# A two-layer hybrid mixer: decay rows through DRAM, and four pieces of work in another order

## The chip, the cores and the metric

The kernel runs on one core of one Trainium2 chip. The metric is device time in microseconds for one execution. The engines named below are PE (TensorE, matrix products), DVE (VectorE), ACT (ScalarE), POOL (GpSimd) and SP (SyncE, which here only issues DMAs).

## The reference

The input is one sequence of 512 tokens with 1024 features. Each of two layers has four attention-like branches of 256 features (FOX with a learned decay, DIL with dilated windows, RET a retention, MLA with low-rank queries and keys), a sigmoid gate of 1024 features for each, an output product, and a gated feed-forward block of 2816. Everything is float32.

```python
def hybrid_mixer(h, w_in, b_forget, ret_gn_gain, mla_q_norm, mla_kv_norm, w_uq, w_ukv, w_gate, w_branch, w_out):
    (fq, fk, fv, ff, dq, dk, dv, rq, rk, rv, rg, cq, ckv, kr) = jnp.split(h @ w_in, IN_OFFSETS, axis=-1)
    log_f = jax.nn.log_sigmoid((ff + b_forget).astype(jnp.float32))
    decay = jnp.cumsum(log_f, axis=1).transpose(0, 2, 1)
    o_a = causal_block_attention(heads(fq, FOX_HEADS), heads(fk, FOX_HEADS), heads(fv, FOX_HEADS),
                                 HEAD_DIM ** -0.5, decay)   # s + decay[query] - decay[key], causal softmax
    o_b = dilated_attention(heads(dq, DIL_HEADS), heads(dk, DIL_HEADS), heads(dv, DIL_HEADS))
    o_c = retention(...)                                     # then a norm over each head, gain, silu(rg)
    o_d = causal_block_attention(q_mla, k_mla, ...)          # q, k from rms_norm(cq) @ w_uq, rms_norm(ckv) @ w_ukv
    branches = jnp.stack([merge_heads(o_a), merge_heads(o_b), o_c, merge_heads(o_d)], axis=2)
    gates = jax.nn.sigmoid(h @ w_gate).reshape(B, S, N_BRANCH, D_MODEL)
    merged = jnp.sum(jnp.einsum('bsnw,nwd->bsnd', branches, w_branch) * gates, axis=2)
    return merged @ w_out

for l in range(2):                                           # reference()
    h = rms_norm(x, g_pre_mix[l])
    x = x + rms_norm(hybrid_mixer(h, ...), g_post_mix[l])
    h = rms_norm(x, g_pre_ffn[l])
    f = (jax.nn.silu(h @ w_ffn_gate[l]) * (h @ w_ffn_up[l])) @ w_ffn_down[l]
    x = x + rms_norm(f, g_post_ffn[l])
```

## The kernel before

All activations stay in SBUF; the weights are streamed from DRAM. A float32 product is made of three products of rounded parts (`mm3`, L527 to L531: high by high, high by low, low by high, 512 tokens wide). Each weight tile therefore goes through three steps: SP loads it into one of three `raw` buffers, ACT rounds it into `whi` (L289 for most of the layer, L404 for the feed-forward's wider tiles), and DVE subtracts to get `wlo` (L290, L405). The conversion runs two units ahead of the products.

The main stream is PE's list of weight products: `latents`, the projections, the gates, the output block, the feed-forward. The branches run beside it as generators: after each 6.5 main products, one step of the branch in progress is taken (a step ends at a `yield`). So a further `yield` in a branch puts 6 to 7 more main products between two of its steps. Inside regions marked as ordered the written order holds; elsewhere a scheduler orders each engine's instructions by the dependencies. PE, DVE, ACT, POOL and SP each run their own list strictly in order: an instruction that waits holds up what is behind it. PSUM has two pools of four banks each, `acc` for the main stream and `b` for the branches and other short work.

The places that the change touches:

- `running_sum` (L982) makes FOX's running sums of the log decay, `cum`, one column for each of four token blocks and four heads, by two fp32 matmuls (L989, L990). `attention` needs each head's sums also as a row along the free axis, the same in all 128 partitions: `spread(h)` makes them with four fp32 matmuls against the identity (L648) into a `b` bank, and ACT copies them to `dk[h]` (L651). `make_bias` (L660, DVE) turns `dk[h]` and `cum` into the bias of one block of scores. Behind it follow L681 (minimum and bias, DVE), L683 (exponential, ACT), L690 and L691 (reciprocal on DVE, product on POOL), and the transposes L698 on PE.
- `group_norm` (L826) is retention's norm over heads: sums by PE (L840), an inverse root in some 13 small DVE steps (`factor`, L538 to L546, L846, L848), five yields, and then transposes of the factors (L858) on PE.
- `latents` (L1180) ends the low-rank product. After the last `ps_d` product (`mm3` into a `b` bank) DVE makes the factors of two small norms from the squares that ACT summed (the norm chain, L1205 to L1212, with one root on ACT, L552), and L1215 to L1219 read the four `acc` banks of the latents token block by token block, scaled by them. The transposes of MLA's preparation (L891, L897) need the result. `next_spread` (ACT's copy L1078) and the conversion of the next two weight tiles (`w_conv`: L289, L290) stand inside the `ps_d` loop.
- `quarter_products` (L488) runs the feed-forward's products as seven groups over quarter blocks, with four banks from one pool: `b` for even, `acc` for odd column groups g. In layer two, `to_tokens` (L1723) turns the residual with transposes into `b` banks (L1729), which ACT copies out (L1732).
- `finish` (L1736) is the down product of layer two and what follows: the last of its seven products (n = 6) runs over 11 tiles of k (steps of two), the first eight for both token halves, the others for one half after the other. Each half then goes through a square sum on ACT (L1817), L1819, a root, and L1830 on DVE, and to DRAM.

## Time and profile before

| | us |
|---|---|
| median of 3 runs | 1676.44 (1675.61 to 1676.55) |
| the profiled execution | 1679.01 |
| its span | 1677.2 |
| PE busy in it | 1649.3 |
| DVE, ACT, POOL busy | 1130.8, 851.0, 358.7 |
| mean granted clock of TensorE | 0.997 |

The profile shows one execution. A timeline row gives the start of a group of like instructions, its duration, engine, line and operation, and in brackets how long the engine had been idle before it and what released it. Products on PE overlap, so the time that one takes from the queue is the distance between two starts and not its printed duration.

### The profile page before, as it was taken

The page shows a single profiled execution, that of the slowest core. Times are in us where ns is not written, and L with a number is a line of the kernel's source. Part 1 is how long each engine was busy: PE and PEld are TensorE (multiplying, and loading weights), DVE is VectorE, ACT ScalarE, POOL GpSimd, SP SyncE. Part 2 cuts the span into 40 slices and gives each one's busy share as a digit, 9 for nine tenths or more (in the row PEclk, how much of TensorE's full clock was granted, in tenths as well). Part 3 has the DMA queues.
Part 4 walks back from the last instruction along what each step waited for, and adds up shares of the span by engine and source line. Part 5 has one row for each costly group of instructions (what it writes and reads, how often), then busy time and mean ns, then how long its engine had stood idle before and what let it go on. Part 6 is the DMA issues. An engine that isn't in the chain of part 4 may idle for free.

```text
span 1677.2 us, 26506 instructions
## 1 busy us (share of the span) xinstructions
PE 1649.3 (98%) x9746; PEld 1463.0 (87%) x9746; DVE 1130.8 (67%) x2165; ACT 851.0 (51%) x1682; POOL 358.7 (21%) x400
## 2 busy tenths in 40 slices
PE   8999999999999999999989999999999999999997
PEld 7898888788899999988878988888888989999876
DVE  6657676556469777762286576766565687777897
ACT  6666554323456555553265665533234565555665
POOL 0244333432130000000122343333321300000000
PEclk9999999999999999999999999999999999999999
DMA  5644225667735777443245452256665247775572
GB/s 205 173 107 139 82 82 175 170 169 182 213 87 144 189 186 184 95 154 99 76 148 160 108 145 76 90 175 168 173 161 178 75 137 191 186 183 153 189 234 92
DMA packets 93698, 248.88 MB, mean 148 GB/s; under 512 B 11521, under 2 KB 23041, under 8 KB 93569
## 3 DMA queue, kind: packets, MB, share of 16 engines
q1 hardware_dynamic: 72768, 205.24, 39.0%
q0 software_dynamic: 20800, 41.95, 13.6%
q8 instruction: 77, 1.26, 0.3%
q14 instruction: 53, 0.43, 0.1%
HBM read 220.93 MB, written 31.46 MB: 150 GB/s over the span
## 4 chain that ended last, share of the span: by engine, by line
PE 89%; DVE 6%; issue 2%; ACT 1%; DMA 1%; POOL 1%; DVEq 0%; SPq 0%; POOLq 0%
PE acc L529 15%; PE acc L530 15%; PE acc L531 15%; PE b L503 4%; PE b L505 4%; PE b L504 4%; PE acc L505 3%; PE acc L504 3%; PE acc L503 3%; PE b L752 2%; PE b L672 2%; PE b L698 1%; PE acc L1891 1%; PE acc L1893 1%; PE acc L1892 1%
## 5 line engine op out<-in xcount | busy, mean ns | idle before, releaser
L529 PE MATMUL acc<-a,whi 128*128 128x512 f32 (+1 forms) x1254 | 485.5, 387 | 0.0
L531 PE MATMUL acc<-a,wlo 128*128 128x512 f32 (+1 forms) x1254 | 475.2, 379 | 0.0
L530 PE MATMUL acc<-a,whi 128*128 128x512 f32 (+1 forms) x1227 | 465.3, 379 | 0.0
L289 ACT CAST whi<-raw 128x512 fp32r<-128x512 f32 (+3 forms) x398 | 214.0, 576 | 346.5 <-PE acc L530 174.7
L290 DVE TENSOR_TENSOR wlo<-raw,whi 128x512 fp32r<-128x512 f32 (+3 forms) x398 | 271.9, 713 | 133.4 <-ACT whi L289 132.7
L531 PEld LDWEIGHTS acc<-a,wlo 128*128 128x128 f32 x1254 | 236.3, 188 | 44.7
L529 PEld LDWEIGHTS acc<-a,whi 128*128 128x128 f32 x1254 | 237.1, 189 | 40.0 <-issue 1.0
L530 PEld LDWEIGHTS acc<-a,whi 128*128 128x128 f32 x1227 | 231.9, 189 | 38.9 <-issue 1.0
L405 DVE TENSOR_TENSOR wlo<-raw,whi 128x1024 fp32r<-128x1024 f32 x132 | 157.8, 1195 | 69.0 <-ACT whi L404 67.3
L404 ACT CAST whi<-raw 128x1024 fp32r<-128x1024 f32 x132 | 135.4, 1027 | 126.6 <-PE b L504 48.0
L503 PE MATMUL b<-a,whi 128*128 128x256 f32 x560 | 158.7, 283 | 0.0
L504 PE MATMUL b<-a,whi 128*128 128x256 f32 x560 | 158.5, 283 | 0.0
L505 PE MATMUL b<-a,wlo 128*128 128x256 f32 x560 | 158.5, 283 | 0.0
L1302 DVE TENSOR_TENSOR a<-acc,a 128x512 f32<-128x512 f32 x64 | 44.1, 689 | 140.0 <-PE acc L531 140.0
L503 PE MATMUL acc<-a,whi 128*128 128x256 f32 x448 | 126.8, 283 | 0.0
L504 PE MATMUL acc<-a,whi 128*128 128x256 f32 x448 | 126.8, 283 | 0.0
L505 PE MATMUL acc<-a,wlo 128*128 128x256 f32 x448 | 126.8, 283 | 0.0
L503 PEld LDWEIGHTS b<-a,whi 128*128 128x128 f32 x560 | 107.5, 192 | 0.2
L504 PEld LDWEIGHTS b<-a,whi 128*128 128x128 f32 x560 | 107.5, 192 | 0.0
L505 PEld LDWEIGHTS b<-a,wlo 128*128 128x128 f32 x560 | 107.5, 192 | 0.0
L333 POOL DMA_DIRECT2D raw<-wts x36 | 32.3, 896 | 345.8 <-DMA raw<-wts 140.6
L521 ACT CAST a<-a 128x512 fp32r<-128x512 f32 (+1 forms) x143 | 76.6, 567 | 51.8 <-DVE a L1094 10.7
(282 smaller groups left out, 3203.6 us busy)
## 6 DMA issues: line engine op xcount, KB each, us to landing
raw<-wts SPq DMA_DIRECT2D x257, 512.0 KB, 3.9
raw<-wts POOLq DMA_DIRECT2D x36, 512.0 KB, 6.9
a<-a SPq DMA_DIRECT2D x120, 128.0 KB, 2.3
sums<-wts POOLq DMA_DIRECT2D x30, 512.0 KB, 6.6
raw<-sums SPq DMA_DIRECT2D x20, 512.0 KB, 4.1
raw<-wts SPq DMA_DIRECT2D x35, 256.0 KB, 2.9
sums<-sums POOLq DMA_DIRECT2D x10, 512.0 KB, 3.7
a<-xT SPq DMA_DIRECT2D x16, 256.0 KB, 6.0
```

What stands on the lines that cost most here:

```text
L289: todo.append(lambda hi=hi, src=src, n=n: nc.scalar.copy(hi[:, :n], src))
L290: todo.append(lambda hi=hi, lo=lo, src=src, n=n: (lo_engine or nc.vector).tensor_sub(lo[:, :n], src, hi[:, :n].bitcast(F32)))
L404: self.nc.scalar.copy(hi, src)
L405: self.nc.vector.tensor_sub(lo, src, hi.bitcast(F32))
L503: mm(o, hi[:, c], x[k][0], start=first, stop=False, skip_group_check=i in (2, 3, 4, 6))
L504: mm(o, hi[:, c], x[k][1], start=False, stop=False, skip_group_check=i in (2, 3, 4, 6))
L505: mm(o, lo[:, c], x[k][0], start=False, stop=k == 3, skip_group_check=i in (2, 3, 4, 6))
L521: nc.scalar.copy(hi, src)
L529: mm(out, w[0], x[0], start=start, stop=False)
L530: mm(out, w[0], x[1], start=False, stop=False)
L531: mm(out, w[1], x[0], start=False, stop=stop)
L1302: nc.vector.tensor_mul(z, ps, self.rB)
```

## The change

`spread(h)` becomes one DMA. `running_sum` makes the sums a second time, as 16 rows of 128 tokens (two more fp32 matmuls, with their operands exchanged), ACT copies them from PSUM, SP writes them to a DRAM tile `cum_rows`, and each head reads its four rows back into all 128 partitions. `running_sum` and the start of FOX's attention get one more `yield` each. `group_norm` waits seven yields and not five. The norm chain of `latents` moves into the `ps_d` loop, ahead of `next_spread` and `w_conv`. In layer two the column groups of the feed-forward exchange `b` and `acc`, and so do the banks of `finish`. In the last product of `finish` the steps from k = 6 on, not from k = 8 on, are held back and run one token half after the other.

```diff
--- before.py
+++ after.py
@@ -52,6 +52,7 @@
 HQ = 3
 OPS = 3
 LATE = 8
+LAST = 6
 AHEAD = 2
 FH = FT // 2
 LAST_K = tuple((k, min(2, FH - k)) for k in range(0, FH, 2))
@@ -643,12 +644,9 @@
         cum = self.cum if kind == FOX else None
 
         def spread(h):
-            ps = self.ps("b")
-            for t in range(4):
-                nc.tensor.matmul(ps[:, 128 * t:128 * t + 128], cum[:, 4 * t + h:4 * t + h + 1].to_broadcast([128, 128]),
-                                 self.con("ident"), start=True, stop=True)
             dk[h] = self.a()
-            self.defer(lambda: nc.scalar.copy(dk[h], ps))
+            rows = self.cum_rows.rearrange("(t h) c -> h t c", h=4)[h:h + 1]
+            nc.sync.dma_start(dk[h].rearrange("p (t c) -> p t c", t=4), rows.to_broadcast([128, 4, 128]))
 
         n = len(items)
         biases = {}
@@ -719,6 +717,7 @@
 
         if kind == FOX:
             spread(0)
+            yield
             yield
             make_bias(0)
         for x in range(n + LG + 2):
@@ -847,11 +846,8 @@
             r = self.rsqrt(v, 8)
             nc.vector.tensor_copy(rw.rearrange("p (g c) -> p g c", c=64), r.unsqueeze(2).to_broadcast([128, 8, 64]))
         self.defer(factor)
-        yield
-        yield
-        yield
-        yield
-        yield
+        for _ in range(7):
+            yield
         rb = self.ps("b")
         for t in range(4):
             ts = slice(128 * t, 128 * t + 128)
@@ -989,7 +985,18 @@
         nc.tensor.matmul(ps[:, 0:16], self.con("tri"), nl, start=True, stop=False)
         nc.tensor.matmul(ps[:, 0:16], self.con("ones"), before, start=False, stop=True)
         self.cum = self.cp.tile([128, 16], F32, tag="cum", name="cum")
-        self.defer(lambda: nc.vector.tensor_copy(self.cum, ps[:, 0:16]))
+        rows = self.ps("b")
+        nc.tensor.matmul(rows[0:16, 0:128], nl, self.con("tri"), start=True, stop=False)
+        nc.tensor.matmul(rows[0:16, 0:128], before, self.con("ones"), start=False, stop=True)
+        self.cum_rows = self.dram.tile([16, 128], F32, tag="cum", name="cum")
+
+        def out():
+            nc.vector.tensor_copy(self.cum, ps[:, 0:16])
+            t = self.a()
+            nc.scalar.copy(t[0:16, 0:128], rows[0:16, 0:128])
+            nc.sync.dma_start(self.cum_rows, t[0:16, 0:128])
+        self.defer(out)
+        yield
         yield
         yield
 
@@ -1198,18 +1205,18 @@
                         nc.scalar.activation(junk[:, 0:n], self.ps_l[t][:, o:o + n], AF.Square,
                                              accum_out=ss[:, c:c + 1])
             if k == (QT1 if l else QT):
+
+                nc.vector.tensor_mul(t8[:, 0:4], self.rT, self.rT)
+                for i, n in ((0, 256), (4, 128)):
+                    nc.vector.scalar_tensor_tensor(v[:, i:i + 4], ss[:, i:i + 4], 1.0 / n, t8[:, 0:4], op0=ALU.mult, op1=ALU.mult)
+                nc.vector.tensor_scalar_add(v, v, RMS_EPS)
+                for _ in self.root(v, f, t8):
+                    pass
+                for i in (0, 4):
+                    nc.vector.tensor_mul(f[:, i:i + 4], f[:, i:i + 4], self.rT)
                 self.next_spread()
                 self.w_conv(self.wi)
             self.mm3(ps_d, (w[0][k], w[1][k]), u[k], k == 0, k == KT - 1)
-
-        nc.vector.tensor_mul(t8[:, 0:4], self.rT, self.rT)
-        for i, n in ((0, 256), (4, 128)):
-            nc.vector.scalar_tensor_tensor(v[:, i:i + 4], ss[:, i:i + 4], 1.0 / n, t8[:, 0:4], op0=ALU.mult, op1=ALU.mult)
-        nc.vector.tensor_scalar_add(v, v, RMS_EPS)
-        for _ in self.root(v, f, t8):
-            pass
-        for i in (0, 4):
-            nc.vector.tensor_mul(f[:, i:i + 4], f[:, i:i + 4], self.rT)
         for t in range(4):
             o, r = self.ps_l[t], self.rT[:, t:t + 1]
             nc.vector.tensor_scalar_mul(cq[t // 2][:, 256 * (t % 2):256 * (t % 2) + 256], o[:, 0:256], f[:, t:t + 1])
@@ -1695,7 +1702,7 @@
                     stt(z[1][:, h0], o, -1.0, z[1][:, h0], op0=ALU.mult, op1=ALU.mult)
                     keep(z[1])
 
-            yield from self.quarter_products(ops, ("b", "acc")[g % 2], {
+            yield from self.quarter_products(ops, ("b", "acc")[(g + (xt is not None)) % 2], {
                 0: copy(0), 1: copy(1), 2: copy(2), 3: after_v, 4: after_r, 5: after_a12, 6: after_a22})
         self.wi = self.q_end
         return hid
@@ -1804,7 +1811,7 @@
                 f, k, nk = todo.popleft()
                 ready.append(f(k, nk))
 
-        chain, other, late = ([self.ps(t), self.ps(t)] for t in ("acc", "acc", "b"))
+        chain, other, late = ([self.ps(t), self.ps(t)] for t in ("b", "b", "acc"))
         banks = (chain, other, late, late, chain, chain, chain)
         e = {}
         y, xt = {}, {}
@@ -1871,7 +1878,7 @@
                     for i in range(nk):
                         beside[n](k + i)
                 held.append((k, nk, ready.popleft(), w))
-                if k >= LATE:
+                if k >= (LATE if n < 6 else LAST):
                     continue
                 self.block(banks[n], held.pop(), (0, 1), first, grouped)
             for t in range(2):
```

The new kernel's line numbers differ by up to seven, and the orders below carry each kernel's own.

PE at the start of FOX in layer one, before (`cum` is the tile of sums, `acc` rows are the main stream):

```order
L530 MATMUL acc<-a,whi 128x512
L531 MATMUL acc<-a,wlo 128x512
L648 MATMUL b<-ct,cum 128x128 x4
L529 MATMUL acc<-a,whi 128x512
L530 MATMUL acc<-a,whi 128x512
L531 MATMUL acc<-a,wlo 128x512
```

and after, behind `running_sum`'s first two matmuls:

```order
L532 MATMUL acc<-a,wlo 128x512
L985 MATMUL b<-sm_1548,ct 128x16
L986 MATMUL b<-sm_2260,ct 128x16
L989 MATMUL b<-ct,sm_1548 16x128
L990 MATMUL b<-ct,sm_2260 16x128
L530 MATMUL acc<-a,whi 128x512
L531 MATMUL acc<-a,whi 128x512
```

The four matmuls of a spread are gone from between the main products, and two wide ones (16 rows by 128) stand behind the two that made `cum`; up to FOX's first scores (L672, now L670) there are 33 main products where there were 21, and up to the first L698 (now L696) 68 where there were 51.

SP at the same place, before:

```order
L1099 DMA a<-a 64x512 x6
L258 DMA raw<-wts 128x512
L258 DMA raw<-wts 128x1024 x2
L258 DMA raw<-wts 128x512
L258 DMA raw<-wts 128x1024 x2
```

and after (`cum<-a` is the write to DRAM, `a<-cum` the broadcast reads of the four heads):

```order
L1106 DMA a<-a 64x512 x5
L997 DMA cum<-a 16x128
L1106 DMA a<-a 64x512
L259 DMA raw<-wts 128x512
L649 DMA a<-cum 128x4x128 x2
L259 DMA raw<-wts 128x1024
L649 DMA a<-cum 128x4x128
L259 DMA raw<-wts 128x1024
L649 DMA a<-cum 128x4x128
```

The write waits for ACT's copy and the first two reads for the write; the reads of the third and fourth head stand behind loads of the main stream.

DVE at the end of `latents` in layer two, before (`sm` names are small tiles, L290 is the weights' subtraction, L1215 the first read of the latents' banks):

```order
L562 TENSOR_TENSOR sm_9098<-sm_9098,sm_9099 128x4
L290 TENSOR_TENSOR wlo<-raw,whi 128x512 x2
L1205 TENSOR_TENSOR sm_9075<-sm_9098 128x4
L1207 SCALAR_TENSOR_TENSOR sm_9073<-sm_9072,sm_9075 128x4 x2
L1208 TENSOR_SCALAR sm_9073<-sm_9073 128x8
L554 RECIPROCAL sm_9074<-sm_9075 128x8
L556 TENSOR_TENSOR sm_9075<-sm_9074 128x8
L558 TENSOR_TENSOR sm_9075<-sm_9075,sm_9073 128x8
L560 TENSOR_SCALAR sm_9075<-sm_9075 128x8
L562 TENSOR_TENSOR sm_9074<-sm_9074,sm_9075 128x8
L1212 TENSOR_TENSOR sm_9074<-sm_9074,sm_9098 128x4 x2
L1215 TENSOR_SCALAR a<-acc,sm_9074 128x256
```

and after:

```order
L1209 TENSOR_TENSOR sm_9062<-sm_9085 128x4
L1211 SCALAR_TENSOR_TENSOR sm_9060<-sm_9059,sm_9062 128x4 x2
L1212 TENSOR_SCALAR sm_9060<-sm_9060 128x8
L555 RECIPROCAL sm_9061<-sm_9062 128x8
L557 TENSOR_TENSOR sm_9062<-sm_9061 128x8
L559 TENSOR_TENSOR sm_9062<-sm_9062,sm_9060 128x8
L561 TENSOR_SCALAR sm_9062<-sm_9062 128x8
L563 TENSOR_TENSOR sm_9061<-sm_9061,sm_9062 128x8
L1216 TENSOR_TENSOR sm_9061<-sm_9061,sm_9085 128x4 x2
L291 TENSOR_TENSOR wlo<-raw,whi 128x512 x2
L1222 TENSOR_SCALAR a<-acc,sm_9061 128x256
```

The chain now stands ahead of the two subtractions (L291 there) and no longer between them and the reads of the banks (L1222 there). In layer one it is the same, and there PE's first `acc` products stand ahead of the transposes L891 (now L887): 18 of them, where there were none.

PE at the first column group of layer two's feed-forward, before:

```order
L530 MATMUL acc<-a,whi 128x512
L531 MATMUL acc<-a,wlo 128x512
L1729 MATMUL b<-ct,a 128x128 x16
L503 MATMUL b<-a,whi 128x256
L504 MATMUL b<-a,whi 128x256
L505 MATMUL b<-a,wlo 128x256
```

and after:

```order
L504 MATMUL acc<-a,whi 128x256
L505 MATMUL acc<-a,whi 128x256
L506 MATMUL acc<-a,wlo 128x256
L1736 MATMUL b<-ct,a 128x128 x16
L504 MATMUL acc<-a,whi 128x256
L505 MATMUL acc<-a,whi 128x256
```

The group's products now write `acc`, and 15 of them stand ahead of the transposes L1729 (now L1736).

## Rows read from the trace of the kernel before

**Rows 1.** The page, part 1: busy us, share of the span, instructions.
```profile
PE 1649.3 (98%) x9746; PEld 1463.0 (87%) x9746; DVE 1130.8 (67%) x2165; ACT 851.0 (51%) x1682; POOL 358.7 (21%) x400
```

**Rows 2.** Waits of PE: us in total, times, longest us.
```profile
PE b L891 <- DVE a L1215: 4.1, 2, 3.1
...
PE b L858 <- DVE a L848: 2.1, 2, 1.5
...
PE b L1729 <- ACT a L1732: 1.4, 1, 1.4
```

**Rows 3.** Timeline, FOX first spread: start us, us, engine, line, operation, count.
```profile
180.91 1.05 PE L648 MATMUL b<-ct,cum 128*128 128x128 f32 x8
...
181.72 0.48 PE L529 MATMUL acc<-a,whi 128*128 128x512 f32 x1
...
182.04 0.39 PE L530 MATMUL acc<-a,whi 128*128 128x512 f32 x1
...
182.27 0.39 PE L531 MATMUL acc<-a,wlo 128*128 128x512 f32 x1
```

**Rows 4.** DMA issues: operation, count, KB each, median us to landing.
```profile
raw<-wts SPq DMA_DIRECT2D x35, 256.0 KB, 2.9
...
a<-tab SPq DMA_DIRECT2D x12, 256.0 KB, 3.9
...
a<-a SPq DMA_DIRECT2D x32, 64.0 KB, 2.0
...
a<-uq SPq DMA_DIRECT2D x4, 256.0 KB, 5.9
...
sums<-a POOLq DMA_DIRECT2D x24, 0.0 KB, 3.6
```

**Rows 5.** Timeline, all engines, FOX's start in layer one.
```profile
183.17 0.71 ACT L289 CAST whi<-raw 128x256 fp32r<-128x256 f32 x2
...
185.83 0.73 DVE L660 SCALAR_TENSOR_TENSOR a<-a,cum,ct 128x128 f32<-128x128 f32 x2
...
191.41 0.38 POOL L691 TENSOR_SCALAR a<-a,sm 128x128 f32<-128x128 f32 x1 [6.73 <-DVE sm L690]
...
193.06 0.30 PE L698 MATMUL b<-ct,a 128*128 128x128 f32 x1
```

**Rows 6.** Timeline, PE and DVE, end of latents in layer one.
```profile
32.99 0.15 DVE L1205 TENSOR_TENSOR sm<-sm 128x4 f32<-128x4 f32 x1
...
34.33 0.39 PE L531 MATMUL b<-a,wlo 128*128 128x512 f32 x1
...
36.02 0.21 DVE L1219 SCALAR_TENSOR_TENSOR sm<-acc,sm,vt 128x4 f32<-128x4 f32 x1
...
36.38 0.47 PE L529 MATMUL acc<-a,whi 128*128 128x512 f32 x1
```

**Rows 7.** Timeline, ACT, DVE and PE, end of latents in layer two.
```profile
867.07 0.58 ACT L1078 COPY a<-b 128x512 f32<-128x512 f32 x1
...
871.55 0.48 DVE L1215 TENSOR_SCALAR a<-acc,sm 128x256 f32<-128x256 f32 x1
...
872.19 0.52 PE L891 MATMUL b<-ct,a 128*128 128x128 f32 x2 [3.09 <-DVE a L1215]
```

**Rows 8.** Windows: stretch, us, PE (x), PEld, DVE, ACT, POOL, PEclk, DMA, GB/s.
```profile
872.70:875.80 3.10, 3.10 (x9) 2.48 (x8) 3.10 (x13) 2.18 (x4) 0.00 (x0) 0.51 0.00 0
...
1374.00:1378.00 4.00, 2.56 (x20) 1.89 (x18) 3.31 (x5) 3.44 (x7) 0.86 (x1) 1.00 0.76 165
```

**Rows 9.** Timeline, DVE, retention's norm steps in layer one.
```profile
294.70 3.43 DVE L542 TENSOR_TENSOR sm<-sm 128x8 f32<-128x8 f32 x1
```

**Rows 10.** Timeline, PE and DVE, first quarter group of layer two.
```profile
1376.14 2.12 PE L1729 MATMUL b<-ct,a 128*128 128x128 f32 x16 [1.44 <-ACT a L1732]
...
1381.01 0.69 DVE L1650 TENSOR_TENSOR a<-a,acc 128x512 f32<-128x512 f32 x1 [3.55 <-ACT a L1642]
```

**Rows 11.** Timeline, DVE, the last steps, after the last matmul.
```profile
1670.66 0.68 DVE L1819 SCALAR_TENSOR_TENSOR a<-acc,a 128x512 f32<-128x512 f32 x1
```

## The prediction

> **What bounds the kernel now.** I read the page's busy times first. PE is busy 1649.3 us of a span of 1677.2 [rows 1], so about 28 us are idle, and a change can only pay by taking work from PE's queue, by closing one of its few waits, or by raising its clock. Then I read PE's waits. The reader is to see that the list is short: the three waits that this change touches are 4.1, 2.1 and 1.4 us [rows 2], 7.6 us in all. What lies on DVE, ACT, POOL or SP costs nothing until PE comes to it, so each part below is priced by the moment at which PE arrives against the moment at which the operand is there. One fp32r product of 512 columns takes PE 0.23 us from start to start (182.04 to 182.27 [rows 3]).
>
> **FOX's running sums: the matmuls that go.** One spread is four fp32 matmuls. It holds PE from 180.91 to 181.72, 0.81 us, and the first product behind it takes 0.32 instead of 0.23 [rows 3]: 0.90 us a spread. There are eight (four heads, two layers): −7.2. The new running_sum adds two fp32 matmuls over 128 columns in each layer. A spread's four are of the same width, so two cost half of 0.81, 0.41 us; they stand right behind two fp32 matmuls that are there already, so no further change of format is paid. Two layers: +0.8. Together **−6.4**. The ACT copies of the spreads go too, but no PE wait hangs on them.
>
> **FOX's running sums: the round trip that comes.** The trace of before has neither this small write nor a broadcast read, so I bound them. ACT's copy of the 16 rows stands right behind the second cast of L289, which ends near 183.9 [rows 5]; the write is issued near 184.1. The nearest row for it is the 64 KB move on the same queue, 2.0 us; the longest for something small is 3.6, on POOL's queue [rows 4]. I take 2.0: the rows are there near 186.1, and SP, which waited for that, issues the first two reads. A read is 256 KB in runs of 512 bytes, four for each partition. The nearest rows of that size are 2.9 for a weight load, 3.9 for a table, and at the far end 5.9 for uq [rows 4]. I take 3.5, between the first two, since the reads go out behind a weight load and in a pair: dk of the first head lands near 189.6. From the first bias (185.83) to the end of POOL's L691 (191.41 + 0.38) the kernel before needs 5.96 us [rows 5], so the first normalised block would be there near 195.6.
>
> When does PE ask for it? Before, the first L698 comes at 193.06 [rows 5] with 51 products between L990 and itself; the order of after has 68. The 17 more are 3.9 us (17 by 0.23); two spreads less are −1.8 and the new pair is +0.4: 195.6. So the two extra yields buy almost exactly what the round trip costs, and the slack is about nothing. Counted in the same way from the order, the second head has some 1.4 us to spare, the third some 0.2 (SP issues its read behind a 512 KB load that waits for a free buffer), and the fourth 2.5. While a bias waits for its dk, DVE's queue stands: behind L660 (658 now) are queued the wlo subtractions of the main stream's weights, two units ahead, and then the reciprocals that POOL needs, so a late read reaches PE at L698 first. I price it at 0.3 a layer, **+0.6**. The ends: at 2.9 us nothing; at 5.9, 2.4 us late on the first and the third head of both layers, +9.6 more. A write of 3.6 alone delays the first head, 1.6 us a layer, +3.2.
>
> A rule speaks to this. The Trainium skill, "DMA: Bandwidth & Descriptors", section "Anatomy of one DMA — SWDGE (gpsimd) path", gives a transfer a fixed part of about 2.0 us beside its bytes at 436 GB/s, which for 256 KB makes an estimate of 2.6 us; by it the term would be 0 and the sum −13.2. It is written for the gpsimd path, and the table loads of this trace take 3.9, so the rows decide here.
>
> **Latents, layer one.** PE ends the ps_d products with the one at 34.33, could go on at 34.56, and starts the first acc product at 36.38 [rows 6]: 1.82 us, with three transposes in it. The norm chain on DVE starts at 32.99, behind two subtractions of L290, and the first token block's last reader of its acc bank is L1219, which ends at 36.23 [rows 6]. The change puts the chain ahead of those subtractions, into time in which DVE waited for ACT; with its 2.2 us gone from behind them, L1219 ends near 34.0 to 34.4, before PE wants the bank. In the order of after PE goes straight from ps_d to acc products, and the transposes stand in fours behind 18 of them. They still cost three times 0.13 us (sixteen take 2.12 [rows 10]): 1.8 less 0.4, **−1.4**. Its ends: −1.8 and −0.6, if ACT's casts come late by the chain's square root.
>
> **Latents, layer two.** Here the transposes stay ahead of the acc products and PE waits 3.09 us until 872.19 [rows 7]. The chain leaves DVE's queue behind the subtractions, but its square root now stands on ACT ahead of the copy of L1078, which began at 867.07 [rows 7]. The chain can't start before the squares that ACT ends just there, and its first steps and the root take some 0.7, so that copy would begin near 867.8; the casts and the subtractions behind it come 0.75 later, so of the chain's 2.1 us about 1.2 are gained: L1215 near 870.4 instead of 871.55, L891 near 871.0. There is a second part. After the wait the granted clock is 0.51 for 3.1 us, that is the lower level, 1.2 GHz, with PE busy throughout [rows 8]: work of 1.6 us at full clock, 1.5 lost. Around the wait of 1.44 us at L1729 the granted clock stays 1.00 [rows 8]. The new wait is 1.8 to 1.9, nearer to that than to 3.09, so I take the clock as held: −1.2 −1.5 = **−2.7**; the other end −1.2.
>
> **Retention's norm steps.** L858 waits 1.5 and 0.6, 2.1 in all [rows 2], for the inverse root; one DVE step of it stretches to 3.43 us [rows 9]. Two more yields put 15 and 18 more products ahead of L858, at least 3.4 us, more than either wait: **−2.1**. The steps behind it come later by as much, and the gate groups that need them are more than a group away. Ends: −2.1 and −1.
>
> **Banks of layer two.** PE waits 1.44 at L1729 for ACT's copies, which free the b banks, and the first group's products, on b too, stand behind [rows 10]. On acc, 15 half-width products (half of 0.23 each, 1.8 us) go ahead of the transposes in the order of after and cover it. But the last of the four acc banks is freed by L1650, which DVE ends at 1381.70 [rows 10]; PE now comes to that bank after 36 half-width products and 16 transposes, 6.2 us after 1374.7, near 1380.9. So 0.8 of the 1.44 comes back: **−0.6**, ends −1.4 and +0.2.
>
> **The last steps.** With six instead of eight kept common, more of the last product is done for one token half first. In the order the first half's last matmul is nine from the end before and after, since it needs the last weights in both, and DVE's L1819 of the second half starts at 1670.66 behind the first half's work [rows 11]. **0**; if that work moved ahead of PE's end, up to −1.3, and if a bank were held, +0.3.
>
> **The sum.** −6.4 + 0.6 − 1.4 − 2.7 − 2.1 − 0.6 + 0 = −12.6. Against the profiled execution (1679.0 us, of which the span is 1677.2) this is 1666.4. That execution lies 2.6 above the median of 1676.4, so the predicted median is **1664 us** (1663.8). A measurement of this kernel can tell about 0.2%, 3.4 us, from no change.
>
> **The rivals.** (a) *The reads land late.* For it: 512-byte runs, a pair of reads at once beside a weight load, and rows up to 5.9 [rows 4]. Against it: the loads of that size from plain rows take 2.9. At 5 us each the first and the third head lose 1.5 in each layer, +6: 1670. (b) *Waits only move.* The latents' clock still falls (+1.5), L1650 gives back all of L1729's wait and more (+1), and latents of layer one keeps 0.9 of its wait behind the casts. For it: each freed PE comes earlier to DVE's subtractions, and DVE is 67% busy [rows 1]. That is +3.4: 1667. (c) *Slower than before.* The same mechanism as (a) alone, at L660: every microsecond of landing over 3.5 costs four, so the gain of 12.6 is gone at 3.5 + 12.6/4 = 6.6 us, and at 7.5 the kernel is 0.2% slower, 1680. For it speaks only that no broadcast read from DRAM is in the trace; against it that uq's 5.9 is as slow as a transfer of that size gets in the rows [rows 4]. The same section of the Trainium skill says that completion can be surprisingly long when a write goes to HBM, as the 16 rows do; by that the write, not the reads, would be late, and the first head alone would pay. No row here shows it. (d) *Part of the change does nothing.* The bank swap trades one wait for another and the last steps stay as they are, as the order already says of them: 1665, inside the forecast.
>
> **How the numbers follow.** The forecast with (d), 1660 to 1667: 0.66. (a) and the far end of (b), 1667 to 1673: 0.25. Between that and 1679.8, which is within 0.2% of before: 0.05. (c): 0.04. So faster 0.91, same 0.05, slower 0.04. The range leaves out about a tenth at either end: below, the sum with the read at 2.9 (−0.6), the last steps paying 1.3 and latents and the swap at their good ends (−0.9), 1661, and a little for what I count from the order; above, rival (a) whole: 1660 to 1670.
>
> **What would show it.** Right: no L648, PE's busy time down by 6 to 7 us, no PE wait at L858 and at the first quarter transposes, L891's wait under 2 us with a granted clock of 1.00 behind it. The reads' row should give 3 to 4 us, the small write about 2. Wrong: a PE wait at FOX's L698 (696 now) of over 1 us, or DVE idle ahead of make_bias released by the DMA; a granted clock of 0.50 in latents of layer two; a wait on the L1650 of more than 1.4.

## The result and the profile after

| | us |
|---|---|
| kernel before, median of 4 | 1676.49 (1675.61 to 1677.97) |
| changed kernel, median of 4 | 1684.68 (1683.56 to 1688.3) |
| ratio, after to before | 1.0051 (1.0037 to 1.0065) |
| its profiled execution, span | 1684.69, 1682.9 |
| forecast | 1664 (1660 to 1670) |

The change makes the kernel slower by half a percent, where a gain of 0.75% was forecast. The first part of the page hardly moved against [rows 1]:

```profile
PE 1648.2 (98%) x9690; PEld 1459.7 (87%) x9690; DVE 1131.5 (67%) x2165; ACT 847.9 (50%) x1676; POOL 353.1 (21%) x400
```

PE is 1.1 us less busy and the span 5.7 longer, so the loss is idle time and slow clock. (By the medians the loss is 8.2: the profiled execution of the kernel before lies 2.5 above its median.) PE's waits (us in total, times, longest) say where:

```profile
PE b L839 <- ACT a L833: 8.5, 2, 4.4
...
PE b L828 <- DVE a L763: 2.1, 2, 1.0
PE b L696 <- POOL a L689: 1.9, 6, 0.5
PE b L751 <- DVE ptl L707: 1.6, 2, 0.8
...
PE b L887 <- DVE a L1222: 1.0, 1, 1.0
...
PE acc L504 <- DVE a L1657: 0.4, 1, 0.4
```

The three waits of [rows 2] are answered: the transposes L858 (now L854) and the first group's transposes L1729 (L1736) are gone from the list, and the latents' L891 (L887) has come down from 4.1 to 1.0. In their place stands a wait that the kernel before did not have at all: 8.5 us at L839, the sums of squares of retention's norm, for ACT's square L833. L828 and L751 are new too. DVE's own waits for DMAs, in the same columns:

```profile
DVE a L1329 <- DMA sums<-a: 13.7, 2, 6.9
...
DVE a L658 <- DMA a<-cum: 10.7, 4, 4.2
```

The timeline of retention in layer one shows the chain that ends at L839 (start, us, engine, line, operation, idle before and releaser):

```profile
281.31 1.04 POOL L334 DMA_DIRECT2D raw<-wts  x1 [7.55 <-DMA raw<-wts]
...
282.07 1.39 POOL L362 DMA_DIRECT2D sums<-a  x2
...
290.92 1.29 DVE L1329 SCALAR_TENSOR_TENSOR a<-a,acc 128x512 f32<-128x512 f32 x2 [6.82 <-DMA sums<-a]
...
292.12 2.51 DVE L291 TENSOR_TENSOR wlo<-raw,whi 128x512 fp32r<-128x512 f32 x2
...
292.96 0.39 PE L532 MATMUL acc<-a,wlo 128*128 128x512 f32 x1
294.56 0.67 DVE L857 TENSOR_TENSOR a<-a,b 128x512 f32<-128x512 f32 x1
...
295.93 0.68 DVE L832 TENSOR_TENSOR a<-a,b 128x512 f32<-128x512 f32 x1
...
296.71 0.63 ACT L833 ACTIVATE a<-a 128x512 f32<-128x512 f32 x1
...
297.39 1.86 PE L839 MATMUL b<-ct,a 128*128 128x2 f32 x8 [4.04 <-ACT a L833]
```

Read it from the top. POOL issues an accumulating load (L334) and behind it the one-element DMA with which `make_sums` begins a block of weight sums; it reads one element of a gate's tile. DVE's merge of that gate, L1329, overwrites the tile and waits 6.8 us until the DMA has landed. Behind the merge stand two weight subtractions, the scale step of retention's first pair (L857) and the centre step of its second pair (L832). The centre step ends at 296.6, ACT squares, and PE, which started its last product at 292.96, gets the operands of L839 at 297.39. In the kernel before, the scale (L861) and centre (L833) steps stood ahead of the merge (L1322) in DVE's list. What PE needed from behind it, the second inverse root, it came to only at 299.4:

```profile
282.52 0.69 DVE L861 TENSOR_TENSOR a<-a,b 128x512 f32<-128x512 f32 x1 [1.04 <-PE b L858]
...
287.47 0.68 DVE L833 TENSOR_TENSOR a<-a,b 128x512 f32<-128x512 f32 x1
...
289.36 1.28 DVE L1322 SCALAR_TENSOR_TENSOR a<-a,acc 128x512 f32<-128x512 f32 x2 [1.21 <-PE acc L530]
```

The wait is paid twice, as the windows show (stretch, us, engines, granted clock, DMA): after it, in both layers (the first and the last row), the granted clock is 0.50, the lower level of 1.2 GHz, while PE is busy throughout. In latents of layer two it is 1.00 behind the shorter wait for L1222, but 0.50 for 3.4 us just ahead of it, in the `ps_d` products.

```profile
299.10:303.50 4.40, 4.40 (x11) 3.46 (x12) 4.09 (x13) 0.00 (x0) 2.15 (x3) 0.50 1.05 147
867.00:870.40 3.40, 3.40 (x10) 2.62 (x9) 1.16 (x7) 3.18 (x16) 0.00 (x0) 0.50 0.37 140
875.00:877.00 2.00, 2.00 (x10) 1.53 (x10) 2.00 (x10) 1.97 (x4) 0.00 (x0) 1.00 0.74 236
1140.50:1143.40 2.90, 2.90 (x8) 2.22 (x8) 2.90 (x3) 0.14 (x1) 2.90 (x3) 0.50 1.12 154
```

A table of lags makes the account complete. I paired each main product of a kernel with the same product of the kernel before, both in their profiled executions, and took the difference of their starts; a step between two columns is what the stage between them cost or gave. The columns are moments of the kernel before, in us.

| kernel | 31 | 120 | 340 | 840 | 928 | 1177 | 1360 | 1410 | 1653 |
|---|---|---|---|---|---|---|---|---|---|
| changed | −0.9 | −2.1 | +3.2 | +3.3 | +1.3 | +7.0 | +7.0 | +5.8 | +5.7 |
| e5, yields alone | −0.9 | −0.9 | +6.7 | +6.7 | +8.2 | +16.9 | +16.9 | +16.8 | +16.8 |
| e3, seven yields alone | −0.5 | −0.5 | −2.3 | −2.3 | −1.1 | −1.7 | −1.7 | −1.7 | −1.7 |
| e11, without FOX | −1.4 | −2.6 | −3.9 | −3.8 | −5.7 | −6.5 | −6.5 | −7.8 | −7.8 |
| e1, private copy | −1.6 | −2.8 | −4.8 | −4.8 | −6.8 | −7.6 | −7.5 | −8.9 | −8.9 |
| e9, sums and read early | −1.1 | −2.4 | −6.3 | −6.2 | −8.8 | −13.3 | −13.2 | −14.5 | −14.6 |

From 31 to 120 lies latents of layer one, from 120 to 340 FOX and retention of layer one, from 840 to 928 latents of layer two, from 928 to 1177 FOX and retention of layer two, from 1360 to 1410 the first column group. In the changed kernel both latents and the first column group gain; the two stages with FOX and retention lose 5.3 and 5.7. (Kernels whose latents are as before, e3, e5 and e12, drift by 1.2 to 1.5 from 840 to 928 against this one execution. Their profiled executions have a stretch of 3.4 us at 0.50 in the `ps_d` products, besides the one behind the long wait; the execution of before lacks it. So that stage is known to no better.)

### The profile page after: what moved, and what is told of

It reads as the page before. It is cut to its first block, busy times and chain, and to the rows that moved or that the text cites. A ratio compares the mean times of both kernels' runs of the same rounds, so it can differ in the third digit from the quotient of the medians.

```text
span 1682.9 us, 26386 instructions
## 1 busy us (share of the span) xinstructions
PE 1648.2 (98%) x9690; PEld 1459.7 (87%) x9690; DVE 1131.5 (67%) x2165; ACT 847.9 (50%) x1676; POOL 353.1 (21%) x400
## 4 chain that ended last, share of the span: by engine, by line
PE 87%; DVE 6%; DMA 3%; issue 2%; ACT 2%; POOL 1%; SPq 0%; DVEq 0%; POOLq 0%; ACTq 0%
PE acc L530 15%; PE acc L531 14%; PE acc L532 14%; PE b L504 4%; PE b L505 4%; PE b L506 4%; PE acc L504 4%; PE acc L506 4%; PE acc L505 4%; PE b L751 2%; PE b L670 2%; PE b L1898 1%; DVE wlo L291 1%; PE b L1900 1%; PE b L1899 1%
## 5 line engine op out<-in xcount | busy, mean ns | idle before, releaser
L290 ACT CAST whi<-raw 128x512 fp32r<-128x512 f32 (+3 forms) x398 | 214.1, 578 | 357.1 <-PE acc L531 179.2
L291 DVE TENSOR_TENSOR wlo<-raw,whi 128x512 fp32r<-128x512 f32 (+3 forms) x398 | 279.4, 732 | 124.9 <-ACT whi L290 124.1
L530 PEld LDWEIGHTS acc<-a,whi 128*128 128x128 f32 x1254 | 237.7, 190 | 40.5 <-issue 1.1
L531 PEld LDWEIGHTS acc<-a,whi 128*128 128x128 f32 x1227 | 232.5, 189 | 39.1 <-issue 1.0
L504 PE MATMUL acc<-a,whi 128*128 128x256 f32 x504 | 142.8, 283 | 0.4 <-DVE a L1657 0.4
L504 PE MATMUL b<-a,whi 128*128 128x256 f32 x504 | 142.7, 283 | 0.0
L505 PE MATMUL b<-a,whi 128*128 128x256 f32 x504 | 142.6, 283 | 0.0
L506 PE MATMUL b<-a,wlo 128*128 128x256 f32 x504 | 142.6, 283 | 0.0
L505 PE MATMUL acc<-a,whi 128*128 128x256 f32 x504 | 142.6, 283 | 0.0
L506 PE MATMUL acc<-a,wlo 128*128 128x256 f32 x504 | 142.5, 283 | 0.0
L334 POOL DMA_DIRECT2D raw<-wts x36 | 32.3, 896 | 343.4 <-DMA raw<-wts 183.7
L504 PEld LDWEIGHTS acc<-a,whi 128*128 128x128 f32 x504 | 96.7, 192 | 0.6 <-DVE a L1657 0.6
L504 PEld LDWEIGHTS b<-a,whi 128*128 128x128 f32 x504 | 96.7, 192 | 0.2
L505 PEld LDWEIGHTS b<-a,whi 128*128 128x128 f32 x504 | 96.8, 192 | 0.0
```

What stands on the lines that cost most here:

```text
L290: todo.append(lambda hi=hi, src=src, n=n: nc.scalar.copy(hi[:, :n], src))
L291: todo.append(lambda hi=hi, lo=lo, src=src, n=n: (lo_engine or nc.vector).tensor_sub(lo[:, :n], src, hi[:, :n].bitcast(F32)))
L504: mm(o, hi[:, c], x[k][0], start=first, stop=False, skip_group_check=i in (2, 3, 4, 6))
L505: mm(o, hi[:, c], x[k][1], start=False, stop=False, skip_group_check=i in (2, 3, 4, 6))
L506: mm(o, lo[:, c], x[k][0], start=False, stop=k == 3, skip_group_check=i in (2, 3, 4, 6))
L530: mm(out, w[0], x[0], start=start, stop=False)
```

## The experiments

**Theory A**: the merge's wait for the one-element DMA is what holds retention up. **Theory B**: the distance on PE between mean and squares is too short whatever the DMA does. **Theory C**: FOX's new reads crowd out that DMA. After the first four experiments **theory D** joined A: what brings the merge ahead of the scale and centre steps is FOX's two extra yields, which put retention 13 main products later against the gate groups. (13 is twice 6.5. Counted in the trace of e6, which has FOX's two yields alone, the mean of the second pair stands behind 15 more main products than in the kernel before.)

**e1_marker_copy.** The one-element DMA reads a copy of its own.

```diff
-                        self.make_sums(3 * l + gi - 1, ("pr", "qv")[dp // 2], z)
+                        mark = self.cp.tile([1, 1], F32, tag="mark%d%d%d" % (l, gi, dp), name="mark")
+                        nc.scalar.copy(mark, z[0:1, 0:1])
+                        self.make_sums(3 * l + gi - 1, ("pr", "qv")[dp // 2], mark)
```

> The new kernel, but the one-element DMA that starts a block of weight sums (make_sums) reads a private copy made by ACT instead of a gate's tile, so the gate's merge L1329 on DVE no longer waits for that DMA; order on DVE and PE else as in the new kernel. Theory A (in the new kernel the merge waits 6.9 us for that DMA, and retention's scale and centre steps, which the extra yields put behind it in DVE's queue, make PE wait at the sums of squares L839, 4.0 and 4.4 us, with a clock at 0.50 for some 4 us behind it): the two waits shrink under 1 us each and the time falls by 8.5 + 4 = 12 to 13, to about 1672. Theory B (too few products between mean and variance, the DMA does not matter): the waits stay, about 1684. Theory C (the reads of cum_rows crowd out the one-element DMA): as A here.

Measured: 1670.49 us, ratio 0.9959 (0.9944 to 0.9974), 14 us below the changed kernel. L839 is no longer among PE's waits. The timeline of the same place:

```profile
281.44 1.39 POOL L362 DMA_DIRECT2D sums<-mark  x2
...
283.29 0.69 DVE L1331 SCALAR_TENSOR_TENSOR a<-a,acc 128x512 f32<-128x512 f32 x1
...
289.13 0.69 DVE L832 TENSOR_TENSOR a<-a,b 128x512 f32<-128x512 f32 x1 [1.14 <-PE b L828]
...
290.55 1.29 POOL L363 DMA_DIRECT2D sums<-wts  x2 [7.73 <-DMA sums<-mark]
```

The DMA lands as late as before (290.55), but the merge (L1331 here) runs at 283.29 and the centre step at 289.13, 6.8 us earlier than in the changed kernel. A holds, B falls.

**e2_four_yields_var.** Four yields instead of two between centre and squares.

```diff
         self.defer(centre)
         yield
         yield
+        yield
+        yield
```

> The new kernel with four yields instead of two between retention's centre step and its sums of squares (L839), so 33 main products instead of 15 stand between mean and variance of the second pair. Theories A, B and C all: PE comes to L839 some 4 us later, no wait there, the clock holds, about 1672. If the waits move on to the transposes L854 or to the gates that take retention's result, it stays near 1680.

Measured: 1679.82 us, ratio 1.0016 (1.0006 to 1.0026): a miss by 8. The wait at the squares (L841 here) is 5.1 instead of 8.5. Its timeline in layer one:

```profile
295.91 5.04 DVE L291 TENSOR_TENSOR wlo<-raw,whi 128x512 fp32r<-128x512 f32 x2 [0.67 <-ACT whi L290]
...
300.87 0.67 DVE L832 TENSOR_TENSOR a<-a,b 128x512 f32<-128x512 f32 x1
...
302.26 1.05 PE L841 MATMUL b<-ct,a 128*128 128x2 f32 x8 [2.01 <-ACT a L833]
```

More products ahead of the squares moved the centre step too: it now stands behind the next pair of weight subtractions, which took 5.04 us there. A later step is later in every queue, not on PE alone.

**e3_before_seven_yields.** The kernel before with seven yields in `group_norm`.

```diff
-        yield
-        yield
-        yield
-        yield
-        yield
+        for _ in range(7):
+            yield
         rb = self.ps("b")
```

> The kernel before with group_norm's seven yields alone; no FOX DMA, no extra yield in FOX. In its order DVE's centre step of the second pair stands behind the merge that waits for the one-element DMA. Theory A: the waits at L858 (2.1) go, but PE waits some 4 to 5 us at the sums of squares in each layer and the clock falls behind it: slower than before by 8 to 12, about 1686. Theory C: without the reads the one-element DMA lands in time, no new wait: about 1674. My forecast's own working: 1674.

Measured: 1675.76 us, ratio 0.9989 (0.9979 to 0.9998). The transposes' waits are gone and no new one is there; the lag falls by 1.8 in layer one and 0.6 in layer two. The merge waits for the DMA 2.0 us in all:

```profile
DVE a L1319 <- DMA sums<-a: 2.0, 2, 1.6
```

So the two yields of `group_norm` alone do what the forecast said of them; by the medians they gain 0.8, by the lags of these two stages 2.4, where 2.1 was forecast. My expectation under theory A was wrong: I had taken the DMA's landing as fixed, and here it landed 3.5 us earlier than in the changed kernel (POOL's next issue starts at 287.4 instead of 290.9), too early to hold anything.

**e4_no_extra_yields.** The changed kernel with none of its extra yields.

```diff
             spread(0)
             yield
-            yield
             make_bias(0)
...
-        for _ in range(7):
+        for _ in range(5):
...
         self.defer(out)
         yield
         yield
-        yield
```

> The new kernel without its extra yields: two instead of three in running_sum, one instead of two at FOX's start, five instead of seven in group_norm. DVE's centre step stands ahead of the merge again, as before. Theory A: no wait at L839, L858 waits 2.1 as before, and FOX's L696 pays for the missing 12 products, 2 to 4 us a layer: about 1670 to 1674. Theory C: L839 still waits, since the reads are there: 1680.

Measured: 1672.38 us, ratio 0.9973 (0.9961 to 0.9985). No wait at the squares, with all the FOX DMAs in place, so C falls. Against the changed kernel, the extra yields cost 12.3 us there. FOX pays for the missing products, and the transposes wait in one layer:

```profile
PE b L696 <- POOL a L689: 3.3, 4, 1.4
...
PE b L853 <- DVE a L846: 1.8, 1, 1.8
```

**e5_yields_no_dma.** The kernel before with all four extra yields and nothing else (the yields of e3 and those that e4 takes out).

> The kernel before with all of the change's extra yields (one in running_sum, one at FOX's start, two in group_norm) and nothing else: the spreads stay matmuls, no cum_rows, latents and banks as before. PE and DVE stand in retention as in the new kernel. Theory D (FOX's two yields put retention 13 main products later against the gate groups, so the loads, the one-element DMA on POOL's queue behind them and the merge come late, and scale and centre stand behind the merge): PE waits some 4 us at the sums of squares in each layer with the clock down behind it, 12 us in all, less the 2.1 of the transposes: about 1686. Theory C (the reads of cum_rows delay the one-element DMA): no such wait, about 1675.

Measured: 1695.8 us, ratio 1.0102 (1.0087 to 1.0117), the slowest of all. PE's waits, and DVE's for the DMA:

```profile
PE b L841 <- ACT a L835: 8.2, 2, 4.3
...
PE b L698 <- POOL a L691: 2.8, 6, 0.7
PE b L830 <- DVE a L765: 2.1, 2, 1.0
```

```profile
DVE a L1321 <- DMA sums<-a: 13.4, 2, 6.7
```

They are those of the changed kernel, with no DMA of FOX in the program. This is the experiment that decides: between the profiled executions the yields cost 16.8 us, and the rest of the change gives back 11 (16.8 less 5.7); by the medians, 17.5 and 9.3. The sign and the place are as expected, the size is not: 10 us more than the 1686. The expectation left out the waits at L698 and L830, and behind each wait at the squares the granted clock was 0.50 for 6.8 us; the miss was not taken apart further.

**e6_new_five_yields.** The changed kernel with five yields in `group_norm`; FOX's stay (the line of e4's diff on `range`).

> The new kernel with group_norm back at five yields; FOX's two extra yields stay. In its order the merge stands ahead of the centre step, the scale step ahead of the merge, and 19 main products lie between mean and variance. Theory D: PE still waits 3 to 4 us at L839 in each layer, about 1682. Rival (the two yields of group_norm are the cause): no wait there, 1 to 2 us at the transposes, about 1672.

Measured: 1684.35 us, ratio 1.0039 (1.0026 to 1.0051), no better than with seven. Its profiled execution is the fastest of six, at 1681.06. In it the wait at the squares is halved and the transposes wait again:

```profile
PE b L839 <- ACT a L833: 4.1, 2, 2.7
...
PE b L854 <- DVE a L847: 1.6, 1, 1.6
```

With e3, the cause among the yields is FOX's pair: without it `group_norm`'s two bring no wait at the squares, with it they add to the wait (8.5 for 4.1) and take away the transposes'.

**e7_early_sums.** `running_sum` one branch earlier, no extra yields in FOX, seven in `group_norm`.

```diff
-            if kind == FOX:
+            if kind == DIL:
                 self.bg.append(("forget", self.running_sum(self.forget(z))))
```

> The new kernel with running_sum run one branch earlier, ahead of DIL's attention, and without the extra yields in running_sum and FOX (group_norm keeps seven). The rows lie in DRAM long before FOX starts, so only the broadcast read stands ahead of the first bias, and retention keeps its place against the gate groups. Theory D: no wait at L839 and at L828, L696 waits 0.5 to 1.5 a layer; the matmuls, latents, the transposes and the banks pay: 1663 to 1666. If the broadcast reads cost more than the write's round trip shows, 1668.

Measured: 1675.82 us, ratio 0.9984 (0.9974 to 0.9993); 10 short of what I expected. Retention is clean, but SP issues the first read only at 184.92, behind FOX's moves of q and k that wait for their sources, and DVE waits 6.0 us for it:

```profile
184.92 0.59 SPq L649 DMA_DIRECT2D a<-cum  x1
...
188.96 0.75 DVE L658 SCALAR_TENSOR_TENSOR a<-a,cum,ct 128x128 f32<-128x128 f32 x2 [6.02 <-DMA a<-cum]
```

**e8_early_and_copy.** e7 with the copy of e1.

> As the run with the early sums, and the one-element DMA reads a private copy (as in the first run). Theory D: the merge waits at most 1.6 us for that DMA there and PE not at all, so nothing more to gain: within 1 us of the early sums. If the one-element DMA still costs somewhere, up to 4 us less.

Measured: 1676.52 us, ratio 0.9988 (0.9979 to 0.9998), the same as e7 within the intervals. In its profiled execution the clock also fell behind the wait at FOX's start: 0.69 is the mean of the 7 us below, in which it was at 0.50 until 200:

```profile
196.00:203.00 7.00, 7.00 (x26) 5.48 (x25) 3.78 (x14) 3.63 (x10) 1.28 (x2) 0.69 0.13 37
```

In e7's profiled execution the clock held there (1.00), and it is 5.4 us shorter. It is also the fastest of e7's ten, so e7's median includes more than the 6.0 us above explain. The clock may be why the runs of both lie several microseconds apart: e7's two fastest have a mean granted clock of 0.997, the other eight 0.994 or 0.995. No profile of the others shows where it fell.

**e9_read_early.** e7 with the first head's read issued in `running_sum`, right behind the write.

```diff
+        self.dk0 = self.a()
+        self.read_rows(0, self.dk0)
...
-            dk[h] = self.a()
-            rows = self.cum_rows.rearrange("(t h) c -> h t c", h=4)[h:h + 1]
-            nc.sync.dma_start(dk[h].rearrange("p (t c) -> p t c", t=4), rows.to_broadcast([128, 4, 128]))
+            dk[h] = self.a() if h else self.dk0
+            if h:
+                self.read_rows(h, dk[h])
```

> As the run with the early sums, but the first head's broadcast read is issued in running_sum, right behind the write and ahead of DIL's attention, not behind FOX's moves of q and k in SP's list. There DVE waited 6.0 to 6.4 us a layer for that read, and PE 3 us a layer behind it. Theory D with that reading: DVE's wait for the first read goes, PE's waits at the first scores and at L696 fall from 3.1 to about 1 a layer, and the time falls by 4 to 6 against the early sums; about 6 to 9 below the kernel before of the same call. If the read is slow whenever issued, no change against the early sums.

Measured: 1664.9 us (1663.64 to 1665.47), ratio 0.992 (0.9905 to 0.9935): 20 us below the changed kernel and faster than the kernel before too. The page, PE's waits in the stages concerned, and DVE's:

```profile
PE 1639.2 (99%) x9690; PEld 1455.4 (88%) x9690; DVE 1138.8 (68%) x2165; ACT 847.5 (51%) x1676; POOL 358.6 (22%) x400
```

```profile
PE b L886 <- DVE a L1226: 1.8, 1, 1.8
PE b L670 <- DVE ptl L707: 1.6, 1, 1.6
...
PE b L696 <- POOL a L689: 1.1, 2, 0.7
```

```profile
DVE a L1333 <- DMA sums<-a: 0.6, 1, 0.6
DVE a L658 <- DMA a<-cum: 0.5, 1, 0.5
```

PE is 10.1 us less busy than in [rows 1]; the bias waits 0.5 us for its reads in all, where it waited 10.7 in the changed kernel.

**e10_read_early_copy.** e9 with the copy of e1.

> As the run with the early read, and the one-element DMA reads a private copy. Theory D: within 1 us of it.

Measured: 1664.19 us, ratio 0.9919 (0.9904 to 0.9933): no more to gain from the copy once retention stands where it stood.

**e11_without_fox.** The kernel before with the latents' chain, the banks and seven yields; no FOX part, `LATE` for all.

> The change without its FOX part and without LAST: the kernel before with the norm chain of latents moved, the banks of layer two exchanged and seven yields in group_norm; spreads by matmul, no extra yields in FOX. Sum of the parts as the curves of lag give them (retention 1.7, latents 3.9, banks 1.3): 6.9 below the kernel before, ratio 0.996. If the parts only pay beside FOX's change, less than 3.

Measured: 1670.12 us, ratio 0.9952 (0.9938 to 0.9967): 7.1 below before, where the lags of the parts had given 6.9.

**e12_before_copy.** The kernel before with the copy of e1 alone.

> The kernel before with the private copy for the one-element DMA and nothing else: a control for the first run. Theory A: in the kernel before, the centre step stands ahead of the merge, so the wait holds up nothing and the time stays within 1.5 us of before. If the copy itself is what gains (by freeing gate tiles elsewhere), 5 or more below before.

Measured: 1678.2 us, ratio 1.0003 (0.9993 to 1.0012). The copy by itself gains nothing; in e1 it removes a wait that only the changed order makes costly.

## Why the prediction was wrong

**The step that failed** is how I costed the extra yields. For FOX the prediction says that "the two extra yields buy almost exactly what the round trip costs" and counts nothing else for them; for retention, that "the steps behind it come later by as much, and the gate groups that need them are more than a group away". I looked at who waits for the late results, and not at which instructions the late steps are queued behind on DVE. The merge L1322 (L1329) stood next behind the centre step in DVE's list before; in the changed kernel, where the second pair stands 24 main products later, the order has the merge ahead, and the merge waits for a DMA. In the kernel before that wait showed as 1.2 us of DVE's idle time, put down to PE, since the DMA landed at the same moment (289.3). A comparison of DVE's order at retention would have shown the swap. Of the working, the term for the yields was −2.1 (the transposes' waits); e5 measures +16.8 for them, and e4 +12.3 beside the rest of the change.

**What made it as large.** Three things add up in each layer: the wait itself, 4.0 and 4.4 us; the slow clock behind it, 6.4 us of work at half speed in layer one (L839's group and products) and 3.4 in layer two, 3.2 and 1.7 lost; and new waits at L828 and L751, 1.0 and 0.8. e1 shows the first two together: without the merge's wait the two stages lose 7.3 and 6.5 us less. That the DMA came later against PE's stream goes back, at least in part, to the same yields. POOL's accumulating load ahead of it needs the plain load that it adds to (L332), and SP held that back for a buffer which a product of retention frees:

```profile
SPq L332 <- PE b L751: 1.3, 1, 1.3
```

Retention stood later. POOL's load starts at 281.31 in the changed kernel and at 280.56 in the kernel before, although the main products were 2 to 3 us ahead there. No run tests this wait by itself.

**Right, point by point.**
- FOX's matmuls and the round trip: −6.4 and +0.6. The landing times were 3.5 us for the reads and 1.8 for the write (DMA, count, KB each, us to landing), where 3.5 and 2.0 were assumed:

```profile
a<-cum SPq DMA_DIRECT2D x8, 256.0 KB, 3.5
...
cum<-a SPq DMA_DIRECT2D x2, 8.0 KB, 1.8
```

  L696 waits 0.17 us at its first block in both layers, where the prediction saw a slack of about nothing. Against e5, which has the same yields, the changed kernel loses 2.3 and 3.0 us less in the two stages from 120 to 340 and from 928 to 1177, 5.3 of the 5.8 forecast. Of the 3.0, up to 1.7 is the clock, which was at 0.50 behind the wait for 6.8 us in e5 and for 3.4 in the changed kernel. A cleaner pair is e9 and e11, with no slow clock in these stages: they differ there by FOX's part alone, in e9 with the early read, and by 6.3.
- Latents, layer one: −1.2, forecast −1.4.
- Latents, layer two: −2.0, forecast −2.7, but not by the terms of the forecast. The wait fell by 2.1, from 3.1 to 1.0, where 1.2 was forecast, and the clock, put at 1.5, gave nothing back. Behind L887 it is 1.00, as assumed; in the `ps_d` products ahead of it, it is 0.50 for 3.4 us, as long as behind the long wait before. PE had waited there for the first weight subtraction. It does so in the kernel before too, whose profiled execution stayed at 1.00 behind it (first the changed kernel, then before):

```profile
PE b L532 <- DVE wlo L291: 1.3, 1, 1.3
PE b L531 <- DVE wlo L290: 1.2, 1, 1.2
```

  The move of the norm chain does not bring this drop, since e3, e5 and e12 have it as well. e9's profiled execution has no drop in latents, waits 1.8 at L886 and gains 2.6 in this stage: the forecast's own case. What decides between the two stays open; that the sum came near in the changed kernel is luck.
- Retention's transposes: their waits went, alone (e3: −1.8 and −0.6) and in the changed kernel.
- Banks: −1.2, forecast −0.6; the wait that was to come back at L1650 (L1657) is 0.35 us, not 0.8.
- The last steps: the lag at 1653 is the lag at 1410 within 0.1, and from PE's last product to the span's end it is 9.0 us before and 8.9 after. Zero, as forecast.

Without the yields' collision the forecast's sum stands: e9, which has every part of the change but keeps retention in its place, runs at 1664.9, 12.3 below its kernel before, where 12.6 was forecast. Its FOX part is another, with the sums one branch earlier and no extra yields, so it does not test the +0.6 of the round trip.

**The signs.** Two of the signs that were to show a wrong forecast did appear: DVE stood idle for the reads ahead of the bias (L658, 10.7 us in all), and the clock was at 0.50 in latents of layer two. The loss lies at neither: L696, which the late reads were to hold up, waits 1.9 us in all and at most 0.5, and for L839 no sign was named. Of the signs of a right one, PE's busy time fell by 1.1 and not by 6 to 7, since work at the lower clock counts as busy for longer.

**The rivals.** None of them was this. "Waits only move" came nearest in kind, but it put the new waits at latents and at the banks and priced them at 3.4; "slower than before" had the right sign by a mechanism that the landing times refute (late reads, 3.5 us, or a late write, 1.8). The chance of 0.04 for slower came from looking for the danger only in what was new in the program.

## What to carry to other kernels

When a step is moved in time, list on each in-order engine what it now stands behind, and give every one of those instructions its own wait; a wait that is invisible because nothing useful was behind it becomes the bound as soon as something is. Buy time for a transfer by issuing it earlier, write and read both, and not by delaying its user: e9 and the changed kernel differ in little else and lie 20 us apart. A marker that reads a live tile through a DMA makes that tile's next writer wait until it has landed: here 6.8 us, as the marker landed just behind the 512 KB load ahead of it on the queue.

## What the runs showed of the hardware

Two DMAs of one element, issued on POOL from 282.1 on, took some 8 us to land, at 290.6 and 290.8, just behind a 512 KB accumulating load issued ahead of them on the same queue (281.3, landed at 290.3); the median of their kind over the run is 3.8. In e3 that load landed at 286.8 and they at 287.1 and 287.4. With PE waits of 4.0 and 4.4 us the granted clock fell to 0.50 for 6.8 and 3.4 us; behind one of 1.0 it stayed at 1.00; behind one of 1.3, with eight matmuls of one column after it, it stayed at 1.00 in the profiled execution of the kernel before and fell to 0.50 for 3.4 us in that of the changed kernel. DVE's weight subtractions, 1.28 us for a pair in most places, took 2.51 in the timeline of the changed kernel and 5.04 in e2. The excess, 1.2 and 3.8, is near the time of the tensor operations that POOL ran beside them: L1330, 1.30, and in e2 L1332 and L523, 1.67 and 1.97. No run tests whether they are the cause.
